# Gate matmuls of a decoder layer's mLSTM issued in blocks of 16, and one store moved to another queue

## The chip, the cores and the metric

The kernel runs on one core of a Trainium2 chip. The metric is the time of one execution in device microseconds (us), given as the median of three runs. A profile of one further execution shows what each engine did and when: TensorE (PE, its weight loads apart as PEld), VectorE (DVE), ScalarE (ACT), GpSimd (POOL) and SyncE (SP), which issues the DMAs.

## What is computed

One decoder layer for 512 positions of width 1024. One input projection feeds a dilated attention branch and an mLSTM branch; both are projected back, merged by sigmoid gates, projected once more and normalised. The change lies in the mLSTM branch:

```python
def mlstm_branch(x_m, z_m, o_m, ...):
    x_c = silu(causal_depthwise_conv(x_m, conv_w, conv_b))        # 512 x 2048
    q = block_diag_proj(x_c, wq)                                  # blocks of 4 x 4
    k = block_diag_proj(x_c, wk)
    v = block_diag_proj(x_m, wv)
    gate_pre = concatenate([q, k, v], axis=-1) @ w_if + b_if      # 8 columns
    li = gate_pre[..., :M_HEADS]
    lf = log_sigmoid(gate_pre[..., M_HEADS:])
    h = mlstm_chunkwise(heads(q), heads(k), heads(v), li, lf)     # 4 heads of 512
    ...
```

and in the very last step, `return rmsnorm(h, norm_out_g)`.

## The kernel before

**Layout.** Activations lie transposed, 128 channels on the partitions and 512 positions along the free axis. The 2048 channels of the mLSTM branch are 16 tiles, numbered `ct`; tile `ct` belongs to head `ct // 4`. A float32 product of full precision is made of three matmuls in the format float32r: each operand is split into a high and a low part (`xh`, `xl`; `whi`, `wlo`), and the product low times low is left out. ACT makes the high part and DVE the low part.

**The loop over tiles.** For each tile the kernel projects the input (24 matmuls into the PSUM tile `xm`; for the first four tiles that is done ahead), copies the result to an SBUF tile `xm`, convolves it on DVE (one `conv<-xm,half` and three `conv<-xm,half,conv`), takes `cth = tanh` on ACT, finishes `conv` on DVE (`conv<-cth,conv`), scales a copy `sx` for later, and splits `conv` into `xch` (ACT) and `xcl` (DVE). Three matmuls give `kp` (the key side, folded with the query weights), which is split into `kph`, `kf` (ACT) and `kpl` (DVE). Ten matmuls then add to the three score tiles `S` of the head; after a head's fourth tile the scores are copied to `sraw`. `xm` and `sx` are also stored to DRAM (`xmd`, `sxd`) and loaded again (`xmr`, `sxr`) when a head needs them: the block of 16 matmuls `v<-Bv,xmr` does so.

**The gate sums.** `q`, `k` and `v` are not built for the gates. GpSimd folds the small weights once into two tables `ust` (`fold_gates`), and each tile adds its share to one PSUM tile `gps` (in the rows: `gates`) by four matmuls with plain float32 operands. Each has 32 output columns and takes one quarter of the array's columns (`tile_position=(0, 32 * i)`): two read `xm` and two read `conv`, each half of the positions. After all 16 tiles, `gsum` adds the quarters up, and a chain of small DVE and ACT steps makes the decay factors that the heads wait for (`aT`, `Abc`).

**What sets the order.** Nothing is issued as the Python code runs. A `Recorder` keeps every call as an operation, with what it reads and writes. `issue` then plays the program through with an estimated cost for each operation (`cost`) and a delay between engines (`LAG`), and gives each engine the ready operation that was recorded first. It does so for a few settings, and `run` issues the order whose end it reckons earliest. The order on each engine is then fixed; an engine waits where an input is late. Calls between `R.together()` and `R.apart()` are one operation, and stay side by side. All calls are issued from one line, so every row says L333.

Tiles in SBUF come from pools with a fixed number of buffers: 51 slots hold nearly all tiles of 512 columns, `xm` and `conv` among them, and a slot is free when its last reader has run.

**The end.** The output is stored in four blocks of 128 positions. In each, DVE scales the second half of the columns and ACT the first half, and two DMAs of 256 KB, both issued by SP, store them.

Of the kernel before, what the change touches and what calls it, by code (L numbers as in the profile page):

```python
# [18 lines left out]
T = 512  # L19
NT = T // P  # L20
# [3 lines left out]
NMT = MW // P  # L24
# [76 lines left out]
class Recorder:  # L101
# [129 lines left out]
    def issue(self, reserve):  # L231

        todo = {}
        for op in self.ops:
            op.users, op.later, op.ready = [], [], 0.0
            todo[op] = len(op.need) + len(op.after)
        for op in self.ops:
            for o in op.need:
                o.users.append(op)
            for o in op.after:  # L240
                o.later.append(op)
        free = dict(self.caps)
        left = {b: b.left for op in self.ops for b in op.bufs}
        pending = {t: list(bs) for t, bs in self.order.items()}
        ready = {e: [] for e in self.ENGINES}
        idle = {e: 0.0 for e in self.ENGINES}
        link, hw = 0.0, 0.0
        events, seq, done = [], 0, []

        def at(t, kind, what):  # L250
            nonlocal seq
            seq += 1
            heapq.heappush(events, (t, seq, kind, what))

        def room(op):
            for b in op.allocs:
                earlier = pending[b.tag].index(b)
                if free[b.tag] < 1 + min(earlier, reserve.get(b.tag, 1 << 30)):
                    return False
            return True  # L260

        for op in self.ops:
            if not todo[op]:
                at(0.0, "ready", op)
        while events:
            now = events[0][0]
            while events and events[0][0] <= now:
                _, _, kind, what = heapq.heappop(events)
                if kind == "ready":
                    heapq.heappush(ready[what.eng], (what.prio, what.idx, what))  # L270
                elif kind == "free":
                    free[what.tag] += 1
            for e in self.ENGINES:
                if idle[e] > now or not ready[e]:
                    continue
                blocked, op = [], None
                while ready[e]:
                    x = heapq.heappop(ready[e])
                    if room(x[2]):
                        op = x[2]  # L280
                        break
                    blocked.append(x)
                    if len(blocked) > 40:
                        break
                for x in blocked:
                    heapq.heappush(ready[e], x)
                if op is None:
                    continue
                for b in op.allocs:
                    free[b.tag] -= 1  # L290
                    pending[b.tag].remove(b)
                done.append(op)
                op.start = now
                end = now + op.cost
                idle[e] = end
                at(end, "idle", e)
                seen = end + 200
                if e == "sync":
                    shape = next(x.shadow.shape for x in op.calls[0][1] if isinstance(x, View))
                    hw = max(hw, now) + 450  # L300
                    begin = max(link, hw + 650)
                    link = begin + max(math.prod(shape) * 4 / 359, 64)
                    seen = link + 900
                for u in op.users:
                    lag = self.LAG.get((e, u.eng), 150)
                    u.ready = max(u.ready, seen if e == "sync" else end + lag)
                    todo[u] -= 1
                    if not todo[u]:
                        at(max(u.ready, now), "ready", u)
                for u in op.later:  # L310
                    u.ready = max(u.ready, now)
                    todo[u] -= 1
                    if not todo[u]:
                        at(u.ready, "ready", u)
                for b in op.bufs:
                    left[b] -= 1
                    if not left[b] and b.tag is not None:
                        at(seen, "free", b)
        if len(done) < len(self.ops):
            return None  # L320
        return max(idle.values()), done
# [16 lines left out]
def hybrid_layer(ctx, tc, a, out):  # L338
    nc = tc.nc
    R = Recorder(nc, a["win"].tensor)  # L340
    V, A, PE, G, SP = (R.engine(e) for e in ("vector", "scalar", "tensor", "gpsimd", "sync"))
# [230 lines left out]
    ust = [slot("ust")[:, :512].rearrange("p (c m) -> p c m", c=NMT) for _ in range(2)]  # L572
# [72 lines left out]

    gps = pv_bank("gates")
    sps = None
    sraw = []
    for ct in range(NMT):
        h, c = divmod(ct, 4)  # L650
        ps = early_ps[ct] if ct < EARLY else proj_t(CXM + ct, "xm")
        if c == 0:
            Mh, Ml = fold_qk(h)
            sps = [sc_bank("S") for _ in range(3)]
        m = slot("xm")[:, :T + 3]
        V.memset(m[:, 0:3], 0.0)
        if ct < EARLY:
            V.tensor_mul(m[:, 3:], ps, rb)
        else:
            A.activation(m[:, 3:], ps, AF.Copy)  # L660
        SP.dma_start(xmd[ct], m[:, 3:])
        if ct == 8:
            block_v(0)
        xc = conv_silu(m, ct)
        ch, cl = split(xc, "xc")
        s = slot("sx")[:, :T]
        V.tensor_scalar(s, xc, hs[:, 16 + ct:17 + ct], None, op0=OP.mult)
        SP.dma_start(sxd[ct], s)
        ps = sc_bank("kp")
        cc = slice(c * P, (c + 1) * P)  # L670
        mm3(ps, Mh[:, cc], Ml[:, cc], ch, cl, True, True)
        kh, kl = split(ps[:, :T - P], "kp", T - P)
        kf = slot("kf")[:, :P]
        A.activation(kf, ps[:, T - P:], AF.Copy)
        if ct == 0:
            fold_gates()
        R.together()
        for i, (w, x) in enumerate(((1, m[:, 3:259]), (1, m[:, 259:515]), (0, xc[:, :256]), (0, xc[:, 256:]))):
            PE.matmul(gps[32 * i:32 * i + 32, :256], ust[w][:, ct, :], x, start=ct == 0, stop=ct == NMT - 1,
                      tile_position=(0, 32 * i))  # L680
        R.apart()
        for j in range(NT - 1):
            t0 = j * P
            ss = slice(t0, t0 + P)
            mm3(sps[j][:, :T - t0], kh[:, ss], kl[:, ss], ch[:, t0:], cl[:, t0:], c == 0, c == 3 and j < 2)
        PE.matmul(sps[2][:, 256:384], kf, xc[:, T - P:], start=False, stop=c == 3)
        if c == 3:
            sr = wide("sraw")
            A.activation(sr[:, 0:512], sps[0], AF.Copy)
            A.activation(sr[:, 512:896], sps[1][:, :384], AF.Copy)  # L690
            A.activation(sr[:, 896:1280], sps[2][:, :384], AF.Copy)
            sraw.append(sr)
# [31 lines left out]
    for t in range(NT):  # L724
        tt = slice(t * P, (t + 1) * P)
# [287 lines left out]
    for t in range(NT):  # L1013
        tt = slice(t * P, (t + 1) * P)
        xr, og = raw_chunk("xr"), raw_chunk("og")
        SP.dma_start(xr, a["x"][tt, :])
        w = T if t < NT - 1 else T // 2
        n = D // w
        ss = [small("so", 1) for _ in range(n)]
        for i in range(n):  # L1020
            cc = slice(w * i, w * i + w)
            ps = mm_bank("out")[:, :w]
            c, o = divmod(w * i, T)
            for d in range(NK):
                mm3(ps, mh[d][:, tt], ml[d][:, tt], woh[d][c][:, o:o + w], wol[d][c][:, o:o + w], d == 0, d == NK - 1)
            V.scalar_tensor_tensor(xr[:, cc], ps, 0.5, xr[:, cc], op0=OP.mult, op1=OP.add)
            junk = slot("junk")[:, :w]
            A.activation(junk, xr[:, cc], AF.Square, accum_out=ss[i])
            if 0 < i < n - 1:
                V.tensor_add(ss[i], ss[i], ss[i - 1])  # L1030
            V.scalar_tensor_tensor(og[:, cc], xr[:, cc], -0.5 * D ** 0.5, go[:, cc], op0=OP.mult, op1=OP.mult)
        v = small("vo", 1)
        V.tensor_scalar(v, ss[n - 1], ss[n - 2], D * EPS, op0=OP.add, op1=OP.add)
        z = rsqrt1(v, "ro")
        A.activation(xr[:, :T], og[:, :T], AF.Copy, scale=z)
        SP.dma_start(out[tt, :T], xr[:, :T])
        V.tensor_scalar(xr[:, T:], og[:, T:], z, None, op0=OP.mult)
        SP.dma_start(out[tt, T:], xr[:, T:])

# [101 lines left out]
```

## Time and profile before

| | |
|---|---|
| three runs | 910.38, 911.08, 912.74 us (median 911.08) |
| the profiled execution's own time | 910.51 us |
| its span, from the first to the last instruction | 908.6 us |
| around the span | 1.9 us |
| PE busy | 888.6 us, 98% of the span |
| DVE, ACT, POOL busy | 576.3, 385.2, 70.2 us |
| mean granted TensorE clock | 0.995 of 2.4 GHz |

Read first how much of the span PE is busy, and then in which stretch it is not. An engine that is busy for part of the span can still set the time of one stretch, if PE waits there for it.

### The profile page before, as it was taken

What the parts mean: (1) busy time and instruction counts of PE and PEld (TensorE: products, weight loads), DVE (VectorE), ACT (ScalarE), POOL (GpSimd) and SP (SyncE); (2) the same over time, 40 slices, a digit from 0 to 9 for tenths busy, and PEclk for the clock granted to TensorE, in tenths of its full rate; (3) what the DMA queues carried; (4) which work ended last, traced back from release to release, by engine and by line L of the source; (5) the groups of instructions that cost most, each with busy time, mean ns of one, the idle gap of its engine ahead of it and who ended that gap; (6) DMA issues with size and microseconds to landing.
All of it is one profiled execution on the core that took longest, in us unless ns stands there. A gap on an engine that the chain in (4) does not pass through costs nothing.

```text
span 908.6 us, 11847 instructions
## 1 busy us (share of the span) xinstructions
PE 888.6 (98%) x4340; PEld 721.9 (79%) x4340; DVE 576.3 (63%) x1154; ACT 385.2 (42%) x724; POOL 70.2 (8%) x136
## 2 busy tenths in 40 slices
PE   7889999999999999999999999999999999999997
PEld 5567777788878888888888888888888888888886
DVE  4999977785429536645855478874777853327533
ACT  7445544543343333332333265654655543325222
POOL 0950100000000000000000111000111100000000
PEclk9899999999999999999999999999999999999999
DMA  8744324242049334204323223312223222224221
GB/s 299 237 148 130 117 97 147 93 140 88 20 157 304 139 116 162 74 19 162 129 70 116 93 82 105 124 62 93 73 91 105 70 75 98 100 98 157 76 80 59
DMA packets 38801, 104.64 MB, mean 115 GB/s; under 512 B 4308, under 2 KB 6100, under 8 KB 38744
## 3 DMA queue, kind: packets, MB, share of 16 engines
q1 hardware_dynamic: 38744, 103.89, 33.5%
q8 instruction: 34, 0.56, 0.2%
q14 instruction: 23, 0.19, 0.1%
HBM read 93.35 MB, written 15.77 MB: 120 GB/s over the span
## 4 chain that ended last, share of the span: by engine, by line
PE 89%; DVE 3%; DMA 3%; issue 1%; POOL 1%; ACT 1%; SPq 1%; DVEq 0%; ACTq 0%
PE zm L333 10%; PE gate L333 10%; PE ym L333 10%; PE om L333 9%; PE xm L333 5%; PE qa L333 5%; PE out L333 5%; PE za L333 5%; PE ka L333 5%; PE va L333 5%; PE ya L333 5%; PE num L333 3%; PE S L333 2%; PE pv L333 2%; PE sa L333 2%; PE pT L333 2%
## 5 line engine op out<-in xcount | busy, mean ns | idle before, releaser
L333 DVE TENSOR_TENSOR wlo<-raw,whi 128x1024 fp32r<-128x1024 f32 (+1 forms) x126 | 150.9, 1200 | 163.3 <-ACT whi L333 163.1
L333 ACT ACTIVATE whi<-raw 128x1024 fp32r<-128x1024 f32 (+1 forms) x126 | 128.1, 1019 | 287.5 <-PE zm L333 75.0
L333 PE MATMUL xm<-xh,whi 128*128 128x512 f32 x128 | 53.1, 419 | 5.5 <-ACT whi L333 5.5
L333 PE MATMUL xm<-xh,wlo 128*128 128x512 f32 x128 | 52.7, 413 | 2.2 <-DVE wlo L333 2.2
L333 PE MATMUL xm<-xl,whi 128*128 128x512 f32 x128 | 52.8, 414 | 2.0 <-DVE xl L333 2.0
L333 PE MATMUL om<-wlo,xh 128*128 128x512 f32 x128 | 50.9, 398 | 0.0
L333 PE MATMUL gate<-xh,whi 128*128 128x512 f32 x128 | 50.9, 397 | 0.0
L333 PE MATMUL zm<-xh,whi 128*128 128x512 f32 x128 | 50.9, 397 | 0.0
L333 PE MATMUL gate<-xl,whi 128*128 128x512 f32 x128 | 50.7, 396 | 0.0
L333 PE MATMUL om<-whi,xl 128*128 128x512 f32 x128 | 50.6, 395 | 0.0
L333 PE MATMUL gate<-xh,wlo 128*128 128x512 f32 x128 | 50.6, 395 | 0.0
L333 PE MATMUL om<-whi,xh 128*128 128x512 f32 x128 | 50.6, 395 | 0.0
L333 PE MATMUL zm<-xl,whi 128*128 128x512 f32 x128 | 50.4, 394 | 0.0
L333 PE MATMUL zm<-xh,wlo 128*128 128x512 f32 x128 | 50.4, 394 | 0.0
L333 PE MATMUL ym<-yl,whi 128*128 128x512 f32 x128 | 50.4, 394 | 0.0
L333 PE MATMUL ym<-yh,wlo 128*128 128x512 f32 x128 | 50.4, 393 | 0.0
L333 PE MATMUL ym<-yh,whi 128*128 128x512 f32 x128 | 50.3, 393 | 0.0
L333 ACT ACTIVATE p<-p,mx 128x128 f32<-128x128 f32 (+1 forms) x64 | 35.4, 556 | 14.3 <-DVE mx L333 14.3
L333 DVE SCALAR_TENSOR_TENSOR conv<-xm,half,conv 128x512 f32<-128x512 f32 x48 | 39.5, 825 | 0.8
L333 DVE CUSTOM_DVE_ANT_0 p<-sa,tb 128x128 f32<-128x128 f32 (+1 forms) x64 | 28.4, 488 | 18.2 <-PE sa L333 18.2
L333 DVE TENSOR_TENSOR ymacc<-ymacc,ym 128x512 f32<-128x512 f32 x24 | 16.5, 688 | 31.2 <-PE ym L333 31.2
L333 PEld LDWEIGHTS xm<-xh,whi 128*128 128x128 f32 x128 | 24.9, 196 | 13.4 <-ACT whi L333 6.2
(253 smaller groups left out, 2218.2 us busy)
## 6 DMA issues: line engine op xcount, KB each, us to landing
raw<-in_win_dram SPq DMA_DIRECT2D x94, 512.0 KB, 3.4
raw<-in_wpb_dram SPq DMA_DIRECT2D x16, 512.0 KB, 3.2
fr<-fd SPq DMA_DIRECT2D x1, 5120.0 KB
xmd<-xm SPq DMA_DIRECT2D x16, 256.0 KB, 4.1
sxd<-sx SPq DMA_DIRECT2D x16, 256.0 KB, 2.0
xmr<-xmd SPq DMA_DIRECT2D x16, 256.0 KB, 5.9
sxr<-sxd SPq DMA_DIRECT2D x16, 256.0 KB, 4.0
tb<-fr SPq DMA_DIRECT2D x16, 256.0 KB, 3.7
```

The lines of the kernel that those rows point to most:

```text
L333: getattr(getattr(self.nc, op.eng), fn)(*a, **k)
```

## The change

The four gate matmuls of a tile are no longer issued with the tile. The tiles are kept in a list, and after a head's fourth tile (`c == 3`) the 16 matmuls of the four tiles are recorded as one operation. So there are four blocks of 16 in place of 16 blocks of four; the matmuls themselves are the same. Apart from that the store of the last block's first half of columns is issued by ACT, which also produces it, and no longer by SP; and the planner takes any `dma_start` for a DMA, whichever engine issues it.

```diff
@@ issue
                 seen = end + 200
-                if e == "sync":
+                if op.calls[0][0] == "dma_start":
                     shape = next(x.shadow.shape for x in op.calls[0][1] if isinstance(x, View))
...
-                    u.ready = max(u.ready, seen if e == "sync" else end + lag)
+                    u.ready = max(u.ready, seen if op.calls[0][0] == "dma_start" else end + lag)
@@ hybrid_layer
     gps = pv_bank("gates")
     sps = None
+    waiting = []
     sraw = []
...
         if ct == 0:
             fold_gates()
-        R.together()
-        for i, (w, x) in enumerate(((1, m[:, 3:259]), (1, m[:, 259:515]), (0, xc[:, :256]), (0, xc[:, 256:]))):
-            PE.matmul(gps[32 * i:32 * i + 32, :256], ust[w][:, ct, :], x, start=ct == 0, stop=ct == NMT - 1,
-                      tile_position=(0, 32 * i))
-        R.apart()
+        waiting.append((ct, m, xc))
+        if c == 3:
+
+            R.together()
+            for ct_, m_, xc_ in waiting:
+                for i, (w, x) in enumerate(((1, m_[:, 3:259]), (1, m_[:, 259:515]), (0, xc_[:, :256]), (0, xc_[:, 256:]))):
+                    PE.matmul(gps[32 * i:32 * i + 32, :256], ust[w][:, ct_, :], x, start=ct_ == 0, stop=ct_ == NMT - 1,
+                              tile_position=(0, 32 * i))
+            R.apart()
+            waiting = []
...
         A.activation(xr[:, :T], og[:, :T], AF.Copy, scale=z)
-        SP.dma_start(out[tt, :T], xr[:, :T])
+        (A if t == NT - 1 else SP).dma_start(out[tt, :T], xr[:, :T])
         V.tensor_scalar(xr[:, T:], og[:, T:], z, None, op0=OP.mult)
         SP.dma_start(out[tt, T:], xr[:, T:])
```

Since the planner makes the order, three places of it follow. The first is PE's order just ahead of the first `kp`, the one of tile 0; the piece is of the difference, with what went and what came.

```order
 L333 MATMUL xm<-xh,wlo 128x512
 L333 MATMUL xm<-xh,whi 128x512
-L333 MATMUL gates<-xm,ust 32x256 x2
-L333 MATMUL gates<-conv,ust 32x256 x2
+L333 MATMUL xm<-xl,whi 128x512
+L333 MATMUL xm<-xh,wlo 128x512
+L333 MATMUL xm<-xh,whi 128x512
 L333 MATMUL kp<-xch,Mh 128x512
 L333 MATMUL xm<-xl,whi 128x512
 L333 MATMUL xm<-xh,wlo 128x512
```

Tile 0's gate block has gone from here, and three projection matmuls of a later tile have moved ahead of the first `kp`.

The second is PE's order of the change where tile 3 is done. `xm_129`, `xm_133`, `xm_137` and `xm_141` are the tiles 0 to 3, `conv_499` to `conv_697` their convolutions, and `gates_758` is the PSUM tile of the sums.

```order
L333 MATMUL xm_715<-xh_433,wlo_524 128x512
L333 MATMUL gates_758<-xm_129,ust_151 32x256 x2
L333 MATMUL gates_758<-conv_499,ust_123 32x256 x2
L333 MATMUL gates_758<-xm_133,ust_151 32x256 x2
L333 MATMUL gates_758<-conv_582,ust_123 32x256 x2
L333 MATMUL gates_758<-xm_137,ust_151 32x256 x2
L333 MATMUL gates_758<-conv_644,ust_123 32x256 x2
L333 MATMUL gates_758<-xm_141,ust_151 32x256 x2
L333 MATMUL gates_758<-conv_697,ust_123 32x256 x2
L333 MATMUL kp_778<-xch_756,Mh_533 128x512
```

The four tiles' matmuls stand in one row, with no other matmul between them; the other three batches look the same.

The third is DVE's order from tile 0's `kpl` to tile 1's `xcl`, for which the second `kp` waits, first before the change (`conv_582` is tile 1, `conv_635` tile 2).

```order
L333 TENSOR_TENSOR kpl_615<-kp_596,kph_608 128x384
L333 SCALAR_TENSOR_TENSOR conv_582<-xm_133,half_161,conv_582 128x512
L333 TENSOR_SCALAR conv_635<-xm_137,half_161 128x512
L333 SCALAR_TENSOR_TENSOR conv_582<-cth_628,conv_582 128x512
L333 SCALAR_TENSOR_TENSOR conv_635<-xm_137,half_161,conv_635 128x512
L333 TENSOR_SCALAR sx_654<-conv_582,hs_167 128x512
L333 TENSOR_TENSOR xcl_657<-conv_582,xch_648 128x512
```

And the same stretch of DVE's order after it (`conv_644` is tile 2).

```order
L333 TENSOR_TENSOR kpl_613<-kp_596,kph_605 128x384
L333 SCALAR_TENSOR_TENSOR conv_582<-xm_133,half_161,conv_582 128x512
L333 TENSOR_TENSOR wlo_626<-raw_473,whi_615 128x1024
L333 SCALAR_TENSOR_TENSOR conv_582<-cth_631,conv_582 128x512
L333 TENSOR_SCALAR conv_644<-xm_137,half_161 128x512
L333 TENSOR_SCALAR sx_650<-conv_582,hs_167 128x512
L333 TENSOR_TENSOR xcl_654<-conv_582,xch_647 128x512
```

A weight split (`wlo`, 1024 columns) now stands ahead of tile 1's `xcl`, and one convolution step of tile 2 has moved behind it. From the gate sums' end on, the order of every engine is nearly as before, and from the second head on it is the same.

## Rows read from the trace of the kernel before

**Rows 1.** The page, busy time, share of the span and instructions of each engine.

```profile
PE 888.6 (98%) x4340; PEld 721.9 (79%) x4340; DVE 576.3 (63%) x1154; ACT 385.2 (42%) x724; POOL 70.2 (8%) x136
```

**Rows 2.** By stretch: us, busy us of each engine, granted clock, DMA share, GB/s.

```profile
30.00:40.00 10.00, 6.16 (x17) 3.17 (x16) 10.00 (x6) 7.90 (x10) 10.00 (x6) 0.82 0.80 270
40.00:50.00 10.00, 9.43 (x34) 6.59 (x33) 10.00 (x9) 2.79 (x4) 10.00 (x10) 0.84 0.19 66
...
60.00:120.00 60.00, 59.53 (x342) 44.83 (x341) 56.07 (x85) 30.11 (x60) 5.90 (x5) 1.00 0.37 124
...
180.00:908.00 728.00, 721.13 (x3515) 597.47 (x3514) 430.95 (x930) 295.38 (x559) 29.49 (x87) 1.00 0.30 104
```

**Rows 3.** Waits of PE from 40 to 180 us: total, times, longest.

```profile
...
PE kp L333 <- DVE xcl L333: 0.3, 1, 0.3
```

**Rows 4.** Timeline of PE at the first gate block: start, duration, idle before.

```profile
54.38 0.39 PE L333 MATMUL xm<-xh,whi 128*128 128x512 f32 x1
54.70 0.63 PE L333 MATMUL gates<-xm,ust 128*32 128x256 f32 x4
57.31 0.63 PE L333 MATMUL gates<-conv,ust 128*32 128x256 f32 x4 [1.98 <-POOL ust L333]
57.87 0.50 PE L333 MATMUL kp<-xch,Mh 128*128 128x512 f32 x1
```

**Rows 5.** Timeline of ACT at tile 0's `xch`.

```profile
56.98 0.63 ACT L333 ACTIVATE xch<-conv 128x512 fp32r<-128x512 f32 x1 [2.04 <-DVE conv L333]
```

**Rows 6.** Timeline of PE at the second gate block, and the second `kp`.

```profile
63.40 0.40 PE L333 MATMUL xm<-xl,whi 128*128 128x512 f32 x1
63.73 0.41 PE L333 MATMUL gates<-xm,ust 128*32 128x256 f32 x2
...
63.97 0.39 PE L333 MATMUL gates<-xm,ust 128*32 128x256 f32 x2
...
64.29 0.50 PE L333 MATMUL xm<-xh,wlo 128*128 128x512 f32 x1
64.63 0.39 PE L333 MATMUL kp<-xch,Mh 128*128 128x512 f32 x1
64.86 0.39 PE L333 MATMUL xm<-xh,whi 128*128 128x512 f32 x1
...
65.55 0.39 PE L333 MATMUL kp<-xcl,Mh 128*128 128x512 f32 x1
```

**Rows 7.** Timeline of PE's weight loads in the fifth gate block.

```profile
84.11 0.11 PEld L333 LDWEIGHTS gates<-xm,ust 128*32 128x32 f32 x2 [0.36 <-issue]
...
84.14 0.12 PEld L333 LDWEIGHTS gates<-xm,ust 128*32 128x32 f32 x2
```

**Rows 8.** Timeline of DVE at tile 1's `xcl`.

```profile
62.34 0.69 DVE L333 SCALAR_TENSOR_TENSOR conv<-cth,conv 128x512 f32<-128x512 f32 x1 [0.30 <-ACT cth L333]
62.95 0.75 DVE L333 SCALAR_TENSOR_TENSOR conv<-xm,half,conv 128x512 f32<-128x512 f32 x1
...
64.00 0.69 DVE L333 TENSOR_TENSOR xcl<-conv,xch 128x512 fp32r<-128x512 f32 x1
...
65.27 1.22 DVE L333 TENSOR_TENSOR wlo<-raw,whi 128x1024 fp32r<-128x1024 f32 x1
```

**Rows 9.** Timeline of SP at the loads of `xmr`.

```profile
100.10 1.83 SPq L333 DMA_DIRECT2D xmr<-xmd  x4
```

**Rows 10.** Timeline of PE at the first `v` block.

```profile
104.03 0.39 PE L333 MATMUL v<-Bv,xmr 128*128 128x128 f32 x2
```

**Rows 11.** DMA issues: KB each, median us from issue to landing.

```profile
xmr<-xmd SPq DMA_DIRECT2D x16, 256.0 KB, 5.9
```

**Rows 12.** Timeline of all engines from 905 us on.

```profile
904.29 0.72 ACT L333 ACTIVATE xr<-og,ro_z 128x512 f32<-128x512 f32 x1 [0.73 <-DVE ro_z L333]
904.76 0.81 SPq L333 DMA_DIRECT2D out_dram<-xr  x2
```

**Rows 13.** By stretch, the last stores (columns as in rows 2).

```profile
905.60:907.10 1.50, 0.00 (x0) 0.00 (x0) 0.00 (x0) 0.00 (x0) 0.00 (x0) 0.89 0.91 344
```

## The prediction

> **What bounds the kernel now.** I read the page's busy times first: PE is busy for 98% of the span, so time is saved only where PE gets less to do or waits less [rows 1]. Then the table by stretch: from 180 us on PE is busy for 721 of 728 us and every other engine has room, and from there the change leaves the orders alone, so what is won before then stays won [rows 2]. The change works between 54 and 172 us. From 60 to 120 us two engines are near their limit, PE with 59.5 and DVE with 56.1 of 60 us [rows 2]. PE's waits tell which of them sets the time: after 60 us PE waits for DVE once, for 0.3 us, until a `kp` has its `xcl` [rows 3]. So PE sets it, but the margin to DVE is thin. The timelines of PE then give the price of a gate block, and what ends the pause ahead of the first `kp` [rows 4, 6].
>
> **The blocks.** One block of four shows its price between matmuls of 512 columns. From the start of the `xm` before it (63.40) to the start of the second matmul behind it (64.63) pass 1.23 us; two plain steps of 0.23 us (64.63 to 64.86) belong to the matmuls around it, so the block costs 0.77 us [rows 6]. Its four matmuls run side by side in two passes, each of which the rows show on its own, 63.73 and 63.97, so a pass takes 0.24 us [rows 6]. Two passes are 0.48 us. The other 0.29 us are paid at entering and leaving a block, not per matmul: `xm` to gates takes 0.33 us in place of 0.23, and two steps behind it are 0.32 and 0.34 us in place of 0.24 and 0.23 [rows 6].
>
> A block of 16 has eight passes and enters and leaves once: 8 x 0.24 + 0.29 = 2.21 us, against 4 x 0.77 = 3.08 us. That would be 0.87 us for each head and 3.5 us in all.
>
> The first block needs care, since it lies in a pause. PE waits there 1.98 us for the table `ust` [rows 4]. That wait goes, yet its length is not won: the `kp` behind it reads `xch`, which ACT finishes at 56.98 + 0.63 = 57.61 us, and `kp` starts at 57.87 [rows 4, 5]. DVE's order up to there is unchanged, so I leave the first `kp` at 57.87. What the pause gives is room for the three `xm` that the new order puts ahead of `kp`: 0.70 us less to do afterwards. From that `kp` on, PE had 15 blocks to do (11.55 us); now it has four batches (8.84 us) and three `xm` fewer: 11.55 - 8.84 + 0.70 = **3.4 us less**.
>
> **The pass inside a batch.** That a third pass follows a second one as closely as the second follows the first is not in the trace, since no tile's block follows another's. From below it costs nothing more. From above, all four weight loads of the next tile lie open: a load takes 0.11 us, and the loads start within 0.04 us of each other [rows 7], so at most 0.15 us at each of the 12 inner borders, 1.8 us. I take nothing: the second pass's loads start at 84.14, 0.03 us after the first pass's, long before its matmuls of 0.4 us are through [rows 6, 7], so the loads already run beside matmuls in the same columns.
> The Trainium skill speaks against the change here: its page "TensorE: Matmul & The Clock Gate", in "Part 3", says that weight loads overlap with matmuls in flight only where their row groups differ, and all four gate matmuls use all the rows. By that rule the borders would cost the 1.8 us and the gain would be 1.6 us; the trace disagrees within a block, with loads 0.03 us apart.
>
> **DVE's margin.** The second `kp` reads tile 1's `xcl`, which ends at 64.69; PE comes there at 65.55, 0.86 us later [rows 6, 8]. Without the second gate block it comes 0.77 us earlier, and 0.1 us is left. On DVE a `wlo` of 1.2 us now stands ahead of that `xcl`, and a `conv` step of 0.75 us and perhaps an idle 0.30 us go [rows 8]: `xcl` ends 0.2 to 0.5 us later. So I expect a new wait of 0.1 to 0.4 us here. On the other side the 0.3 us wait at a later `kp` may go [rows 3], since less else is asked of PE and DVE just there. I take the two as equal, 0 in sum, with bounds of +0.5 and -0.3 us.
>
> **The store.** SP issues the last two stores one behind the other, 0.81 us for both [rows 12]. ACT can issue its half as its own work ends (905.01), where SP began on it about half of 0.81 us after 904.76, 0.15 us later. This ends nothing sooner: from 905.6 to 907.1 the DMA engines are 91% busy at 344 GB/s, and at that rate the 512 KB of both halves take 1.5 us [rows 13]. The first half's issue still starts that stretch. So I take 0. ACT issues no DMA in this trace, so I bound it by SP's issue of 0.4 us to either side. ACT has nothing else left to do.
> The Trainium skill's page "Trainium Kernel Development and Optimization", under "Key Constraints", says that queues of different engines share the same 16 DMA engines and that issuing from several saves only the issue time. By that the store would be worth up to 0.4 us and the sum 3.8; the trace, with its engines full, leaves nothing of it.
>
> **Sum.** 3.4 us less PE work, 0 for waits, 0 for the store. The profiled execution would come to 910.51 - 3.4 = 907.1 us (span 905.2). It lies 0.57 us below the median of the runs, and I forecast the median: 911.08 - 3.4 = **907.7 us**, 0.37% less. About 0.3% (2.7 us) is what a measurement of this kernel tells from no change, so faster means below 908.35 and slower above 913.8.
>
> **Rivals.**
> *DVE takes the early gain back.* If PE waits for DVE as much as it saves until tile 7 is through, the first two batches give nothing. PE would then keep what the others bring: of the 3.4 us, 7 x 0.77 - 2 x 2.21 + 0.70 = 1.7 us are lost, 909.4. For it speak DVE's 56 of 60 us and the margin of 0.1 us [rows 2, 8]; against it that PE lost only 0.3 us to DVE so far [rows 3] and keeps projection matmuls to fill in. Chance 0.08.
> *Weight loads lie open at the inner borders.* 1.8 us of the gain go, 909.5. Rows 7 speak against it. Chance 0.05.
> *The clock falls in the pause.* The new pause is unbroken, from 54.38 + 3 x 0.23 + 0.39 = 55.5 to 57.87, 2.4 us, where it is 1.98 us today [rows 4]. At 30 to 50 us, with PE busy for 6.2 of the first 10 us, the granted clock went to 0.82 and 0.84 of 2.4 GHz [rows 2], so part of the time ran at 1.2 GHz. The same again would cost (0.18 + 0.16) x 10 = 3.4 us: 911.1. Against it: today's pause left the clock at 1.00 [rows 2], and PE now works longer just before. Chance 0.05.
> *Slower: PE waits at the `v` block.* Each tile's `xm` and `conv` now hold two of the 51 slots until the batch has run, and slots feed the loads of `xmr`. Those were issued from 100.10, and `v` began at 104.03, 3.9 us later [rows 9, 10]; the median load takes 5.9 us [rows 11]. If they can start only at the second batch's end, PE has 21 matmuls left before `v` (11 of 512 columns, four each of 384 and 256, two in two float32 passes), some 18 full steps or 4.1 us. So the wait is up to 1.8 us by the median, 909.5. It is slower than before from a landing 7.5 us after the batch, and by more than 0.3% from 10.2 us, which asks for the load to queue behind a whole weight chunk that waits for DVE. Chance that it goes so far 0.04; up to 1.8 us is in the next item.
> *More is won*, 906.2: DVE gets ahead, the waits go, and the store gives 0.4 us. Chance 0.06.
> My forecast has what is left, 0.72, with 906.8 to 908.9 of its own (waits -0.3 to +0.5, the store, and 0.6 us between a single run and a median).
>
> **The numbers.** Faster: 0.06, and 0.64 of the forecast's 0.72; 0.70. Same: its other 0.08, DVE, loads and clock, 0.26. Slower: 0.04. The range, 906.4 to 909.6, holds the forecast and the two cases near 909.5, and leaves out the clock, the slow case and the ends.
>
> **What would show it.** Right: four runs of 16 gate matmuls, passes 0.24 us apart throughout, 2.2 us each; no wait for `ust`; the first `kp` still near 57.9 after a pause of about 2.4 us; `gsum` 3.4 us earlier than today, and the same shift at every later stage; the last landing moved by no more than that. Wrong: gaps inside a batch, at every second pass; new PE waits for `xcl` or `kpl` before 100 us, or for `xmr`; a clock below 1.00 after 58 us; a shift that shrinks after 180 us, which would mean that a later stage is not bound by PE.

## The result, and the profile after

The change is faster, by half a per cent. On one chip, with six executions of each, the kernel before took 911.0 us and the changed one 907.0 us (medians). The ratio is 0.9948, with a 95% interval of 0.9936 to 0.9960; it is close to that of the means, 906.51 and 911.27 us, while the medians differ by only 4.0 us. Of the 911.08 us of before the ratio makes 4.7 us (3.6 to 5.8). The forecast was 3.4 us less, so it had the sign and was 1.3 us short; scaled, the result is 906.3 us and lies 0.1 us below the forecast's range. One execution of e3c further down, 1469.22 us at a mean granted clock of 0.558, is left out of its ratio.

The profiled execution of the change took 907.21 us, with a span of 905.2. The page's busy times answer to [rows 1], and the table by stretch to [rows 2]:

```profile
PE 886.7 (98%) x4340; PEld 727.1 (80%) x4340; DVE 576.0 (64%) x1154; ACT 385.8 (43%) x724; POOL 71.5 (8%) x136
```

```profile
30.00:40.00 10.00, 6.67 (x19) 3.71 (x17) 9.97 (x6) 7.87 (x11) 10.00 (x7) 0.77 0.67 238
40.00:50.00 10.00, 9.53 (x32) 7.58 (x32) 10.00 (x10) 2.64 (x4) 10.00 (x10) 0.72 0.27 97
...
60.00:120.00 60.00, 59.68 (x343) 48.41 (x342) 54.91 (x85) 30.05 (x58) 6.01 (x4) 0.98 0.34 120
180.00:905.00 725.00, 718.69 (x3506) 596.00 (x3506) 427.68 (x925) 292.86 (x555) 29.32 (x86) 1.00 0.31 104
```

PE does less (886.7 for 888.6 us) and is no less bound. One entry is new: from 60 to 120 us the granted clock is 0.98, where it was 1.00.

PE's waits from 40 to 180 us, the first rows; the wait of [rows 3] for `xcl` is gone, and so is that of [rows 4] in the gate block. The wait for `aT` is not new: the kernel before has it as well (0.6 us), just behind 180 us.

```profile
PE kp L333 <- ACT xch L333: 2.3, 2, 1.9
PE aT L333 <- DVE aa L333: 0.5, 1, 0.5
```

The first row holds two waits. One is the pause ahead of the first `kp`; the other, 0.32 us, is at a much later one, and the second `kp` (tile 1's) is reached without a wait. Two rows of PE's timeline:

```profile
66.50 0.39 PE L333 MATMUL kp<-xcl,Mh 128*128 128x512 f32 x1
...
118.82 0.50 PE L333 MATMUL kp<-xch,Mh 128*128 128x512 f32 x1 [0.32 <-ACT xch L333]
```

The timeline of PE at the first `kp`, for [rows 4]:

```profile
55.73 0.40 PE L333 MATMUL xm<-xh,whi 128*128 128x512 f32 x1
58.08 0.50 PE L333 MATMUL kp<-xch,Mh 128*128 128x512 f32 x1 [1.95 <-ACT xch L333]
58.42 0.39 PE L333 MATMUL xm<-xl,whi 128*128 128x512 f32 x1
...
60.00 0.63 PE L333 MATMUL xm<-xl,whi 128*128 128x512 f32 x1
60.42 0.63 PE L333 MATMUL xm<-xh,wlo 128*128 128x512 f32 x1
60.85 0.63 PE L333 MATMUL xm<-xh,whi 128*128 128x512 f32 x1
```

Up to 58.4 us this is what the prediction described: an unbroken pause, and a first `kp` at 58.1. Then steps of 0.43 us follow, where the same matmuls take 0.23. The table of three short stretches shows the granted clock beside them (the last four columns are POOL's busy time, granted clock, DMA share and GB/s):

```profile
57.00:59.00 2.00, 0.92 (x4) 0.61 (x5) 2.00 (x5) 0.63 (x1) 0.00 (x0) 1.00 0.77 232
59.30:62.60 3.30, 3.30 (x10) 2.62 (x9) 2.92 (x5) 2.55 (x5) 0.00 (x0) 0.50 0.24 94
62.80:65.00 2.20, 2.20 (x14) 1.98 (x13) 2.20 (x5) 0.64 (x1) 0.00 (x0) 1.00 0.64 203
```

The clock was granted at 1.2 GHz from 59.3 to 62.6 us, and PE got through 10 matmuls there. Before it, PE had stood still for 1.95 us.

The timeline of PE at the first batch, for [rows 6] (each row holds the two matmuls on one operand; the gates of `conv` are left out):

```profile
76.62 0.40 PE L333 MATMUL xm<-xh,wlo 128*128 128x512 f32 x1
76.95 0.41 PE L333 MATMUL gates<-xm,ust 128*32 128x256 f32 x2
...
77.19 0.39 PE L333 MATMUL gates<-xm,ust 128*32 128x256 f32 x2
...
77.41 0.38 PE L333 MATMUL gates<-xm,ust 128*32 128x256 f32 x2
...
77.62 0.38 PE L333 MATMUL gates<-xm,ust 128*32 128x256 f32 x2
...
78.48 0.39 PE L333 MATMUL gates<-xm,ust 128*32 128x256 f32 x2
...
78.81 0.50 PE L333 MATMUL kp<-xch,Mh 128*128 128x512 f32 x1
79.15 0.39 PE L333 MATMUL kp<-xcl,Mh 128*128 128x512 f32 x1
```

Only the first step from pass to pass is 0.24 us. The six from 77.19 to 78.48 take 1.29 us, 0.215 each, at the borders between tiles (77.19 to 77.41) as within them. From 76.62 to 79.15 pass 2.53 us; without two plain steps of 0.23 the batch costs 2.07.

At the end, the last rows of ACT, SP and ACT's queue, for [rows 12]:

```profile
900.90 0.72 ACT L333 ACTIVATE xr<-og,ro_z 128x512 f32<-128x512 f32 x1 [0.73 <-DVE ro_z L333]
901.37 0.33 SPq L333 DMA_DIRECT2D out_dram<-xr  x1
901.65 0.37 ACTq L333 DMA_DIRECT2D out_dram<-xr  x1
```

From the end of ACT's work (901.62) to the end of the span pass 3.6 us, as before (905.01 to 908.6).

### The profile page after: what moved, and what is told of

It is laid out like the page before. It is cut to its first block, busy times and chain, and to the rows that moved or that the text cites. A ratio compares the mean times of both kernels' runs of the same rounds, so it can differ in the third digit from the quotient of the medians.

```text
span 905.2 us, 11844 instructions
## 1 busy us (share of the span) xinstructions
PE 886.7 (98%) x4340; PEld 727.1 (80%) x4340; DVE 576.0 (64%) x1154; ACT 385.8 (43%) x724; POOL 71.5 (8%) x136
## 4 chain that ended last, share of the span: by engine, by line
PE 93%; DVE 4%; issue 1%; ACT 1%; DMA 1%; SPq 0%; DVEq 0%; ACTq 0%
PE zm L333 10%; PE gate L333 10%; PE ym L333 10%; PE om L333 9%; PE xm L333 8%; PE out L333 5%; PE qa L333 5%; PE za L333 5%; PE ka L333 5%; PE va L333 5%; PE ya L333 5%; PE num L333 3%; PE S L333 3%; PE pv L333 2%; PE sa L333 2%; PE pT L333 2%
## 5 line engine op out<-in xcount | busy, mean ns | idle before, releaser
L333 DVE SCALAR_TENSOR_TENSOR conv<-xm,half,conv 128x512 f32<-128x512 f32 x48 | 37.2, 775 | 0.8
```

What stands on the lines that cost most here:

```text
L333: getattr(getattr(self.nc, op.eng), fn)(*a, **k)
```

## The experiments

Each ratio is against the kernel before on the same chip. The median of a job's executions of before was 911.2 to 912.0 us.

**Which edit.** e1 is the kernel before with the store's move (and the planner's new test for a DMA); e2 is the change without it.

```diff
...
-        SP.dma_start(out[tt, :T], xr[:, :T])
+        (A if t == NT - 1 else SP).dma_start(out[tt, :T], xr[:, :T])
```

> The kernel before with the store's half on ScalarE's queue and the planner's new test for a DMA, and nothing else. My theory: the stretch from the last work of ACT to the end of the span stays 3.56 us, so the time stays within 0.3 us of before, 911. Rival: the store brings part of the gain, up to 0.4 us less, 910.6.

> The change without the store's move. My theory: the batches bring the whole gain, 907.0 like the change, at most 0.3 us beside it. Rival: the store gave up to 0.4 us, 907.4.

e1: 911.41 us, ratio 0.9999 (0.9990 to 1.0007). e2: 907.04 us, 0.9947 (0.9933 to 0.9960). The store brings nothing that can be measured, and the batches all of it. e2's profiled execution took 905.92 us, with the clock at 1.00 after 40 us, so it shows the change without the fall of the clock. From the first `kp` to the first `num`, where the order is the old one again, PE took 134.96 us before and 130.25 us in e2, 4.7 us less.

**The clock.** e3 fills the pause of the change with eight matmuls that do no useful work.

```diff
...
+        if ct == 0:
+            R.ops[-3].extra = [("matmul", (ps, Mh[:, cc], xh[0]), dict(start=True, stop=True))] * 8
```

(`R.ops[-3]` is the first `kp`; calls in `extra` are issued ahead of it and unknown to the planner.)

> The change, with eight extra matmuls of 512 columns ahead of the first kp, into its own PSUM tile, which the kp then overwrites. They do no useful work and take the time in which PE stood still. My theory: the pause of 1.95 us makes the clock fall to half from 59.3 to 62.7 us, and that costs 1.6 us (the steps from 59.21 to 62.80 summed against their usual lengths); with the pause filled there is no granted clock of 0.5 after 58 us, the first kp stays at 58.1, and the time is 1.3 to 1.9 us under that of the change, 905.4. Rival: the clock falls for another reason (the chip's own swing from run to run, or the start of the kernel), the stretch at 0.5 stays or the time does not move: 907.0.

905.46 us, 0.9932 (0.9919 to 0.9944), 1.6 us under e2 on the same chip, at the first theory's number. The timeline of PE and the stretch that ran at half clock in the change:

```profile
56.34 2.02 PE L333 MATMUL kp<-xh,Mh 128*128 128x512 f32 x8
58.38 0.50 PE L333 MATMUL kp<-xch,Mh 128*128 128x512 f32 x1
```

```profile
59.30:62.60 3.30, 3.30 (x19) 2.63 (x18) 3.08 (x5) 2.60 (x5) 0.00 (x0) 1.00 0.30 115
```

19 matmuls fit where 10 did, though the first `kp` came 0.3 us later. From the first `kp` to the first `num` pass 131.55 us in the change, 130.25 in e2 and 130.20 in e3, so the fall cost the profiled execution of the change 1.3 us. Filling the pause won 1.6 us by the medians of e2 and e3, and 1.4 by their ratios.

What makes the clock fall is known less well. Five profiles have the batches and an unfilled pause. Four of them show the fall: the change, e5, e6 and e7 (the last three below), behind pauses of 1.95, 2.30, 1.96 and 2.31 us. e2 does not, though its pause is as long. Its first `kp`, and its stretch:

```profile
58.03 0.50 PE L333 MATMUL kp<-xch,Mh 128*128 128x512 f32 x1 [2.29 <-ACT xch L333]
```

```profile
59.30:62.60 3.30, 3.30 (x19) 2.62 (x18) 3.08 (x5) 2.69 (x5) 0.00 (x0) 1.00 0.21 82
```

With the pause filled (e3, and further down e4, both e10 and e11) the clock stays at 1.00 there in all five profiles. It does so too behind the pauses of 1.86 to 1.98 us of the kernel before, in its four profiles and e1's. So the fall comes behind an unfilled pause, but the length of the pause alone does not decide it.

How many executions without a profile have the fall can only be guessed from their mean clock. Of the eleven of the change and e2, eight had a mean clock of 0.990 to 0.992 and took 906.94 to 907.23 us; three had 0.994 to 0.996 and took 904.75 to 906.04. The five of e3 had 0.993 to 0.996 and took 905.22 to 906.35. That suggests a fall in eight of eleven, but the mean also holds what the clock does before 50 us, and e11, with its pause filled, has an execution at 0.992 that took 904.61.

e3c is the control: the same eight matmuls in the pause of the kernel before, into `gps` ahead of its first block.

> The control to the eight extra matmuls: the kernel before with eight such matmuls ahead of its first gate block, in the pause of about 2 us that it has there. No profile of the kernel before shows the granted clock below 1.00 after that pause. My theory: there is nothing to win, within 0.3 us of before. Rival: filling a pause with matmuls helps by itself, whatever the clock does, then 1.5 us less than before, as in the change.

910.51 us, 0.9987 (0.9978 to 0.9996): 1.2 us less, against my theory and nearer to the rival's 1.5. So the kernel before loses something to its pause as well. The ten executions that count took 910.01 to 911.01 us, and 12 of the 15 of before on that chip took longer than the slowest of them. To see the loss, the kernel before was profiled three times more.

> The kernel before, unchanged, one more profiled execution. My theory: where the execution is above 911.3 us, the granted clock is 0.5 for some 3 us right after the first kp, as in the change; where it is below 910.8 us, the clock stays at 1.00 there. Rival: the clock stays at 1.00 after 58 us in every execution, and the spread has another cause.

> The kernel before, a second further execution: by my theory a granted clock of 0.5 after the first kp where it takes over 911.3 us and 1.00 where it takes under 910.8; by the rival 1.00 in any case.

> The kernel before, a third further execution: by my theory a granted clock of 0.5 after the first kp where it takes over 911.3 us and 1.00 where it takes under 910.8; by the rival 1.00 in any case.

They took 911.31, 910.70 and 910.63 us, all with the clock at 1.00 after 58 us. The slowest of them started late: its first `kp` came at 59.09 us, the others' at 58.06 and 58.12. The stretch from 60 us of the slowest:

```profile
60.00:120.00 60.00, 59.66 (x344) 45.11 (x343) 56.36 (x85) 30.32 (x60) 5.90 (x5) 1.00 0.38 127
```

So part of the spread is the start, as the rival has it. No execution over 911.31 us was profiled, and what filling its pause gave the kernel before stays open: that filling a pause helps whatever the clock does is not ruled out there.

**The price of a border.** e6 puts a matmul over the whole array between the tiles of each batch; e7 puts the same twelve behind the first batch and ahead of the others. They go into the unused half of `gps`.

```diff
             for ct_, m_, xc_ in waiting:
+                if ct_ % 4:
+                    PE.matmul(gps[:, 256:512], xh[0][:, :P], xh[0][:, :256], start=False, stop=False)
```

> The change, with one extra matmul of 256 columns (128 rows and columns, into the unused half of the gates' PSUM tile) between the tiles of each batch, twelve in all. They add 12 x 0.12 = 1.4 us of work of their own. My theory: each makes PE leave the 32-column tiles and enter them again, 0.29 to 0.31 us more each: 1.4 + 12 x 0.3 = 5.0 us over the change, about 912. Rival: entering and leaving is not what costs; then as with the matmuls put together, 1.4 us over the change, 908.4.

> The control to the kernel before this one: the same twelve extra matmuls of 256 columns, three to a batch, but all behind the first batch and ahead of the other three, so that they open no border. My theory and the rival alike: 1.4 us over the change, 908.4. The difference to the kernel with them between the tiles is the price of twelve borders: 3.6 us by my theory, about 0 by the rival.

e6: 912.27 us, 1.0010 (1.0002 to 1.0019). e7: 908.33 us, 0.9967 (0.9956 to 0.9979). They differ by 3.9 us, where 3.6 were expected. The timeline of PE in e6, from the last pass of one tile to the second of the next:

```profile
76.60 0.39 PE L333 MATMUL gates<-xm,ust 128*32 128x256 f32 x2
...
76.93 0.39 PE L333 MATMUL gates<-xh 128*128 128x256 f32 x1
77.24 0.41 PE L333 MATMUL gates<-xm,ust 128*32 128x256 f32 x2
...
77.48 0.39 PE L333 MATMUL gates<-xm,ust 128*32 128x256 f32 x2
```

From pass to pass over the border are 0.64 us in place of 0.215: 0.12 for the extra matmul, 0.3 for leaving and entering. The next pass takes 0.24 again, 0.02 more than inside a batch, so twelve borders come to 12 x 0.33 = 4.0 us, near the 3.9 measured. The timeline of PE in e7, at the three extra matmuls ahead of a batch:

```profile
131.16 0.51 PE L333 MATMUL gates<-xh 128*128 128x256 f32 x3
131.60 0.41 PE L333 MATMUL gates<-xm,ust 128*32 128x256 f32 x2
```

They cost what they are long, 3 x 0.12 us, and the pass behind them follows after one entry of 0.1. It is the number of changes between 32-column tiles and the whole array that is paid, not the matmuls in between.

**Batches of two tiles.**

```diff
-        if c == 3:
+        if c % 2 == 1:
```

> Batches of two tiles, eight of them, in place of four batches of four tiles. My theory: each entering and leaving costs 0.29 us and each pass 0.215 to 0.24, so a batch of eight matmuls costs 0.33 + 0.69 + 0.31 + 0.34 - 0.46 = 1.20 us, eight of them 9.6 against 4 x 2.06 = 8.25: 1.4 us over the change, 908.4 (906.9 where the clock does not fall at the first kp). Rival: the place of the blocks behind a head's four tiles, not their number, brings the gain: then no step between before and the change by number, anything from 907 to 911.

910.98 us, 0.9997 (0.9988 to 1.0005), 2.6 us more than expected. Its eight batches cost what was worked out (prices of 1.2 us by their starts), so it is not the batches. From the first `kp` to the first `num` its profiled execution needs 4.5 us more than e2 (134.73 for 130.25). The dearer batches are 1.4 of that. The clock was at half after the pause (0.50 from 58 to 60 us), which lengthened the steps by about 1.9 us in sum; PE waited 0.6 us for `xcl`; and the steps of the first `v` block took 4.21 us where they take 3.49 in e2. At the end the last DMA's issue was 1.4 us longer (below). As a test of the dose it failed, and by its time alone the rival, that the number of batches does not matter, stands; the prices in the trace speak against it.

**Useful work in the pause.** e4 moves the `xm` matmuls up PE's order by eight places from the first `kp` on, over 29 of them, so that eight useful ones fill the pause. e10 does it over 53 and 101.

```diff
...
+        xs = [o for o in done[k:] if getattr(o, "name", "") == "xm"][:29]
+        at = [done.index(o) for o in xs]
+        for i, o in zip(at, xs[8:]):
+            done[i] = o
+        for i in reversed(at[-8:]):
+            del done[i]
+        done[k:k] = xs[:8]
...
```

> The change, with the xm matmuls moved up PE's order by eight places from the first kp on, over 29 of them: eight useful matmuls stand where PE stood still, and eight fewer stand behind the 29th. My theory: as with the eight extra matmuls, 1.6 us by the clock, and on top up to 1.87 us (8 steps of 0.23) for work that is already done, as far as DVE keeps up: 903.5 to 905.4, the gates' sum 3.2 us earlier than in the change if all is kept. Rival: DVE takes back what PE saves before 120 us, then it is no better than the extra matmuls, 905.4 (or 907.0 if the clock is not the cause).

> The change with the xm matmuls moved up by eight places from the first kp on, as in the kernel over 29 of them, but over 53, so that the eight places that fall free lie behind the tile projected next, at about 82 us in place of 70. My theory: over 29, PE stood waiting for xch and xcl between 66 and 77 us, 1.8 us, because DVE sets the time there; from 77 to 85 us DVE has 1 us of 8 to spare, so about half is kept: 904.5 to 905.0. Rival: DVE sets the time up to 120 us, and nothing is kept: 905.8.

> The same over 101, so that the eight places fall free at about 110 us, where DVE has 1 us in 11 to spare and more from 120 us on. My theory: the 1.87 us are kept, 903.6 (up to 0.7 us more if DVE is late once more), with the first half of the gates' sums as in the change and gsum 1.9 us earlier than with the eight extra matmuls. Rival: nothing is kept, 905.8.

905.86, 905.69 and 905.66 us, with ratios of 0.9933, 0.9933 and 0.9934: no better than matmuls without use. The 1.9 us of work done ahead are lost again each time, as the rival said. The waits of PE, from its timelines in e4, e10 over 53 and e10 over 101:

```profile
69.39 0.49 PE L333 MATMUL kp<-xch,Mh 128*128 128x512 f32 x1 [0.68 <-ACT xch L333]
70.25 0.50 PE L333 MATMUL kp<-xcl,Mh 128*128 128x512 f32 x1 [0.36 <-DVE xcl L333]
```

```profile
84.42 0.50 PE L333 MATMUL kp<-xch,Mh 128*128 128x512 f32 x1 [1.16 <-ACT xch L333]
```

```profile
102.72 0.50 PE L333 MATMUL S<-xch,kph 128*128 128x512 f32 x1 [0.58 <-ACT kph L333]
110.49 0.50 PE L333 MATMUL kp<-xcl,Mh 128*128 128x512 f32 x1 [0.29 <-DVE xcl L333]
116.63 0.50 PE L333 MATMUL kp<-xch,Mh 128*128 128x512 f32 x1 [0.50 <-ACT xch L333]
```

Wherever the eight places fall free, PE waits there for what ACT and DVE make of `conv` and `kp`; these waits are 1.0, 1.2 and 1.4 us, the larger part of the 1.9. From `kp` to `num` the three take 130.24, 130.18 and 129.88 us, against 130.20 in e3. So PE's neighbours have no 1.9 us to give before 117 us.

**Better versions.** e9 holds the folding of `ust` back and uses two batches of 32; e11 is e10 over 101 with the scaling of `sx` on ACT.

```diff
-        if c == 3:
+        if ct % 8 == 7:
...
-        if ct == 0:
+        if ct == 3:
+            held, R.hold = R.hold, (R.ops[-1],)
             fold_gates()
+            R.hold = held
```

> A try at a better version: two batches of 32 matmuls (tiles 0 to 7 and 8 to 15), and the folding of the tables ust held back until tile 3's kp in the plan, since nothing needs it before the first batch. In the change GpSimd folds from 40 to 57 us, and DVE's conv steps take 0.95 us there against 0.75 later. My theory: DVE paces PE up to about 75 us (the kernel with eight moved xm matmuls gained nothing over the one with eight extra ones), so with DVE undisturbed the first kp comes 1 to 2 us earlier, and two batches fewer save 2 x 0.35 us: 903.5 to 905. Rival: the folding then disturbs DVE later, where it paces PE as well, or slots held longer make PE wait: 905.5 to 908.

917.10 us, 1.0069 (1.0056 to 1.0082), 6 us slower than before; the theory was wrong, and so was the rival's 905.5 to 908. The first `kp` did come 6.4 us earlier (51.66) than in the change, but in the planner's new order PE then runs short of work. By stretch:

```profile
50.00:60.00 10.00, 6.25 (x25) 4.09 (x23) 10.00 (x20) 3.61 (x6) 0.00 (x0) 0.93 0.49 169
60.00:70.00 10.00, 8.10 (x30) 6.19 (x30) 9.90 (x19) 5.22 (x11) 1.26 (x2) 0.73 0.27 88
70.00:80.00 10.00, 8.59 (x39) 6.30 (x38) 9.90 (x14) 4.75 (x9) 5.11 (x5) 1.00 0.55 191
```

PE is idle for 7 of 30 us while DVE is full, and the clock is low for part of that time.

```diff
...
-        V.tensor_scalar(s, xc, hs[:, 16 + ct:17 + ct], None, op0=OP.mult)
+        A.activation(s, xc, AF.Copy, scale=hs[:, 16 + ct:17 + ct])
```

> The change, with the scaling of sx done by ACT in place of DVE (16 x 0.48 us off DVE), and eight xm matmuls moved into the pause, with the places falling free 101 xm later. My theory: DVE took back the moved work; with DVE relieved PE keeps it, 903.5 to 904.7. Rival: something else than DVE takes it back (ACT's steps, which now get longer, or the weights), 905.5 or more.

904.79 us, 0.9926 (0.9912 to 0.9940). It is the fastest, below both kernels, but its interval overlaps that of e10, and the planner's order changed with it. From `kp` to `num` it takes 129.13 us, where e10 over 101 takes 129.88. That relieving DVE brought the 0.7 us between their ratios is likely and not shown.

## Why the prediction was right and wrong

**What bounds the kernel: right for the change, with less room than I said.** PE set the time, and the gain lasted: `gsum` came 3.6 us earlier (167.28 for 170.92), the first `gate` 3.4 (714.95 for 718.32), the end of the span 3.4. But DVE is as near its limit as PE until 117 us (e4, e10).

**The blocks: the mechanism right, the pass mis-sized.** "A pass takes 0.24 us" was the step that failed. It is true of the first step of a block, the only one that the trace of before has, and I carried it to the six that follow, which take 0.215. A batch costs 2.07 us and not 2.21, so the four give 0.6 us more. The enter-and-leave price of 0.29 us held: 0.3 in e6.

**The pass inside a batch: right.** No weight load lies open, and nothing is lost at the inner borders. By the rule that the prediction cites from the Trainium skill's "TensorE: Matmul & The Clock Gate", "Part 3", the borders would have cost 1.8 us; the trace, with 0.215 us over a border as within a tile, disagrees with that rule. The same part also lets a load into the background weight buffer go ahead of matmuls in flight, and the trace does not speak against this. What its page "TensorEngine Tiling (Array Packing)" says under "Key Properties", that changing the tiling mode drains TensorE, agrees with e6.

**DVE's margin: the sum right, the place wrong.** At the second `kp` no wait came. In e2 tile 1's `xcl` ends at 64.81 us and PE takes it up at 65.11; in the change these are 65.08 and 66.50, with PE held up by the clock. The 0.3 us wait of [rows 3] is gone, and a new one of 0.3 us for `xch` came near 118 us (118.82 in the change, 117.47 in e2), which I had not named. So the two cancel as forecast, but that they do is luck.

**The slower rival went the other way.** `v` does not wait for `xmr` in the change. It had waited in the order of before: 0.4 us in e1, by its waits of PE,

```profile
PE v L333 <- DMA xmr<-xmd: 0.4, 1, 0.4
```

and the 32 steps of the first `v` block took 3.79 us before and 3.49 in e2. The prediction asked about this wait for the change alone. It differs between executions: in four more profiles with the order of before, those of p1 to p3 and e3c, the steps took 3.4 to 3.8 us.

**The clock: judged too unlikely.** I gave the fall 0.05, and it came in four of the five profiles with the batches and an unfilled pause. It cost the change 1.3 us and not 3.4: I had taken the two slices of 10 us at 30 to 50 us as its measure.

**The sum: 3.4 us forecast, 4.7 measured where the clock stayed up.** From the first `kp` to the first `num` e2 takes 4.7 us less than before. By the passes the forecast's 3.4 becomes 4.0. My term "0 for waits" left out the rest of what the trace shows: 0.3 us at the `v` block, and 0.2 in PE's two waits for `aT`, on the chain behind `gsum` (0.6 and 0.3 us before, 0.5 and 0.2 in e2). That makes 4.5; the last 0.2 us I cannot place.

**The executions.** The profiled ones differ by 3.3 us: e2's gain, less 1.3 us of fall. That this is just my 3.4 is two errors that cancel. The means differ by 4.8 us, since the six executions of before lie on average 0.8 us above its profiled one, and the six of the change 0.7 below theirs. So the other executions of before lose something that its profile at 910.51 us does not show. Its pause has a part in it, as filling it won 1.2 us; whether its clock falls there was not caught in a profile and stays open.

**More is won: the size came, the reason did not.** The time of 906.3 us is that of this rival (906.2), to which I gave 0.06. But the store gave nothing, and the parts to which I gave a size, 0.3 us of waits and 0.4 of the store, make 907.0 and not 906.2.

**The store: right.** e1's ratio alone could not tell 0 from 0.4 us, but the stretch from the end of ACT's work to the end of the span is 3.6 us with the store on either queue.

## What to carry to other kernels

Where few small matmuls use a part of the array, collect them: what is paid is each change from the whole array to the tiles and back, 0.3 us here, and only the first pass behind it is slow. When work is taken out ahead of a wait, look at the pause that it leaves: behind 1.95 us of it PE ran at 1.2 GHz from 59.3 to 62.6 us, and even useless matmuls in it won 1.6 us. One profile does not tell how often that happens: e2, with a pause of 2.29 us, kept its clock. And before moving work into such a pause, read how full the next engine is. Here PE lost all of it again, waiting for DVE and ACT.

## What the hardware showed that was not expected

ACT's issue of the last store took 0.37 or 0.38 us in all profiles that have it but one; in e5's it took 1.77, and the end of the span came 7.8 us after the start of the last matmul in place of 6.8:

```profile
904.60 1.77 ACTq L333 DMA_DIRECT2D out_dram<-xr  x1
```

DVE's steps are longer while GpSimd works. In e9, where GpSimd rests from 45 to 63 us, a `conv<-cth,conv` takes 0.68 us at 50.03, and 0.95 at 79.06, where GpSimd folds; in the change, with GpSimd folding, it takes 0.93 at 56.43. And half a clock costs nothing where PE isn't the bound: at 40 to 50 us the granted clock was 0.72 in the change and 1.00 in e2, and the first `kp` came at 58.08 and 58.03.
